# Residual and branch sum of a streaming-encoder layer: vector adds against accumulating DMAs

## The chip, the cores and the metric

The kernel runs on one core of one Trainium2 chip. A core has a matrix engine (TensorE, in the profile PE, with PEld for its weight loads), a vector engine (VectorE, DVE), a scalar engine (ScalarE, ACT), GpSimd (POOL), and SyncE (SP), which here only issues DMAs. They run side by side, each through its own queue in order, and wait for each other on semaphores. Matmul results land in PSUM, everything else lives in SBUF (128 partitions), inputs and outputs in HBM. The metric is the device time of one execution in microseconds.

## The reference

One layer of a hybrid encoder over 1024 prompt frames and 32 sample frames, 1056 tokens of 1024 features, all in float32:

```python
h = rmsnorm(x, g_mix)
q, k, v, cb, cc, cx, ga, gc = split(h @ w_in)
y_attn = attend(q, k, v) @ w_attn_out
y_conv = (cb * causal_conv(cc * cx)) @ w_conv_out
merged = sigmoid(ga) * y_attn + sigmoid(gc) * y_conv     # the sum of the two branches
x = x + merged @ w_o                                     # the residual of the output projection
f = square(relu(rmsnorm(x, g_ffn) @ w_up)) @ w_down
x = x + f
x = x + sigmoid(rmsnorm(x, g_ple) @ w_ple_gate) * (p @ w_ple)
y = rmsnorm(x, g_final)
```

Keys, values and the last convolution rows are outputs as well.

## The kernel before

All activations are held transposed: a row block is 128 features on the partitions by 1056 tokens, and there are KD = 8 such rows of the model width. A float32 matmul is made of three passes: operands are split into a high part (a cast on ScalarE) and a low part (a subtraction on VectorE), and high x high, high x low and low x high are accumulated in PSUM. The tokens are taken in three thirds of 352 columns (`ts`), one PSUM bank each.

Stages in order: input projection, attention, the branch projections, the output projection, the MLP up and down, the gated embedding. The change lies in the branch projections (`branches`, line 1022) and the output projection (`output_projection`, line 1401).

`branches` goes over 14 units, the list SEQ_B: c2, a0, c3, a1, c4, a2, c5, a3, c6, a4, c7, a5, a6, a7, where a is the attention branch, c the convolution branch and the number is the row. (c0 and c1 were done during attention.) A unit loads its weights and its gate two units ahead (`branch_fetch`, SP's queue), splits the weights one unit ahead (`branch_high` on ScalarE, `branch_low` on VectorE), runs three groups of 12 matmuls, one for each third (`branch_group`), and multiplies each group by the gate out of PSUM (`branch_post`, line 939, VectorE). The gates of most rows are scaled and put through a sigmoid a unit ahead (`branch_scale`, on GpSimd for c and on VectorE for a; `branch_sigmoid`, ScalarE). The third group of a unit is multiplied during the next unit.

When both branches of a row n are there, that is in the unit after a_n, the row is merged: `merge_add` adds the attention tile into `mg[n]`, `merge_high` casts the sum into `mh[n]`, `merge_low` makes `ml[n]`. The last row is merged in thirds, the first two of them in the last unit. The output projection then reads `mh` and `ml` of all eight rows.

`output_projection` goes over the 8 output rows, with three groups of 24 matmuls each (`wo_group`, lines 1379 to 1381); for row 0 the contributions of input rows 0 to 6 come first, those of row 7 at the end. `wo_fetch(n)` (SP's queue) loads the weights and the residual rows of x two rows ahead, `wo_post` adds the residual to each group out of PSUM, and `wo_after` stores the finished row (SP), makes the operands of the MLP (`operands`: two scalings on ScalarE, two subtractions on VectorE), squares the row (ScalarE) and adds the square to a running sum (GpSimd). `wo_sums` builds sums of two rows for the MLP's Strassen-like products and stores them (SP).

The order of instructions on TensorE, ScalarE, VectorE and GpSimd is the order of the calls inside a hand-ordered block; `branches` and `output_projection` stand in one such block. The order of SP's queue, and how neighbouring blocks meet, is left to a scheduler when the program is built. Tiles of a row come from a common pool of 34 buffers (`blk`), which are reused when their last reader is done.

Of the kernel before, what the change touches and what calls it, by code (L numbers as in the profile page):

```python
# [17 lines left out]
KD = D // P  # L18
# [4 lines left out]
NTT = 3  # L23
# [25 lines left out]
def tile_step(  # L49
# [8 lines left out]
    nc = tc.nc  # L58
# [7 lines left out]
    def blk(name, dt=F32, shape=None):  # L66
        return bpool.tile(shape or [P, T], dt, tag="B", name=name)

    ts = [slice(t * TT, (t + 1) * TT) for t in range(NTT)]
# [26 lines left out]
    def raw_w(w, n, kb, name):  # L96
        raw = wraw.tile([P, kb, P], F32, tag="raw", name=f"raw_{name}")
        nc.sync.dma_start(raw, w[n])
        return raw
# [36 lines left out]
    add, sub = ALU.add, ALU.subtract  # L136
    dve, pool = nc.vector.tensor_tensor, nc.gpsimd.tensor_tensor
# [5 lines left out]
    def group(name, n=TT):  # L143
        if spare_ps:
            return spare_ps.pop(0)[:, :n]
        p_ = pools[turn[0] % len(pools)]
        turn[0] += 1
        return p_.tile([P, 384], F32, tag="g", name=name)[:, :n]
# [26 lines left out]
    def prepare_plain(s_, i):  # L175
        w = load_w(None, 0, KD, f"{s_}_{i}", raw=raws[s_][i])
        ws.setdefault(s_, {}).update(zip(("A21", "A22") if i else ("A11", "A12"), even_odd(w)))
# [714 lines left out]
    full = [slice(0, T)]  # L892
    oh, ol, mg, mh, ml = [], [], [], [], []

    fetched, made = {}, {}

    def branch_fetch(b):
        nm, n = b
        w = raw_w(w_conv_out if nm == "c" else w_attn_out, n, 4, f"o{nm}{n}")
        sg = blk(f"s{nm}{n}")  # L900
        nc.sync.dma_start(sg, gd[n + (8 if nm == "c" else 0)])
        fetched[b] = w, sg

    def branch_high(b):
        nm, n = b
        hi = wsp.tile([P, 4, P], F32R, tag="whi", name=f"whi_o{nm}{n}")
        nc.scalar.copy(hi, fetched[b][0])
        made[b] = hi

    def branch_low(b):  # L910
        nm, n = b
        lo = wsp.tile([P, 4, P], F32R, tag="wlo", name=f"wlo_o{nm}{n}")
        dve(lo, fetched[b][0], made[b].bitcast(F32), op=sub)
        made[b] = made[b], lo
# [4 lines left out]
    def branch_scale(b):  # L919
        if gate_ready(b):  # L920
            return
        sg = fetched[b][1]
        (pool if b[0] == "c" else dve)(sg, sg, rs, op=ALU.mult)

    def branch_sigmoid(b):
        if gate_ready(b):
            return
        nc.scalar.activation(fetched[b][1], fetched[b][1], AF.Sigmoid)

    def branch_group(b, t):  # L930
        nm, n = b
        if t == 0 and nm == "c":
            mg.append(blk(f"mg{n}"))
        made[b, t] = ps = group(f"ps_o{nm}{n}_{t}")
        gemm(ps, made[b], 0, *((ch, cl) if nm == "c" else (oh, ol)), ts[t])

    def branch_post(b, t):
        sg = fetched[b][1][:, ts[t]]
        dve(mg[b[1]][:, ts[t]] if b[0] == "c" else sg, made.pop((b, t)), sg, op=ALU.mult)

    def merge_add(n, c):
        dve(mg[n][:, c], mg[n][:, c], fetched["a", n][1][:, c], op=add)

    def merge_high(n, c):
        if len(mh) == n:
            mh.append(blk(f"mh{n}", F32R))
            ml.append(blk(f"ml{n}", F32R))
        nc.scalar.copy(mh[n][:, c], mg[n][:, c])

    def merge_low(n, c):  # L950
        dve(ml[n][:, c], mg[n][:, c], mh[n][:, c].bitcast(F32), op=sub)
# [70 lines left out]
    def branches():  # L1022

        seq = SEQ_B
        for i, b in enumerate(seq):
            prev, nxt = seq[i - 1] if i else None, seq[i + 1] if i + 1 < len(seq) else None
            if i + 2 < len(seq):
                branch_fetch(seq[i + 2])
            else:
                wo_fetch(i + 2 - len(seq))  # L1030
            done = prev and prev[0] == "a"
            if nxt:
                branch_high(nxt)
            else:
                wo_high(0)
            branch_group(b, 0)
            if prev:
                branch_post(prev, 2)
            if done:
                merge_add(prev[1], full[0])  # L1040
                merge_high(prev[1], full[0])
            if nxt:
                branch_scale(nxt)
                branch_low(nxt)
                branch_sigmoid(nxt)
            else:
                wo_low(0)
            if done:
                merge_low(prev[1], full[0])
            branch_group(b, 1)  # L1050
            branch_post(b, 0)
            if nxt is None:
                merge_add(b[1], ts[0])
                merge_high(b[1], ts[0])
                merge_low(b[1], ts[0])
            branch_group(b, 2)
            branch_post(b, 1)
            if nxt is None:
                merge_add(b[1], ts[1])
                merge_high(b[1], ts[1])  # L1060
                merge_low(b[1], ts[1])
# [19 lines left out]
    place, done = min(hooks), 0.0  # L1081
# [27 lines left out]
    with tc.manual_schedule(engines=MM):  # L1109
        nc.scalar.preload_act_table_set("sqrt_and_others")  # L1110
        run(first_gates())
        for s_ in range(2, len(SETS)):
            nm, n = SETS[s_]
# [239 lines left out]
    def fetch_up(s_):  # L1353
        fetch_pair(f"u{s_}", w_up, 2 * s_)

    wo, xs = {}, {}

    def wo_fetch(n):
        xs[n] = blk(f"xr{n}")
        wo[n] = raw_w(w_o, n, KD, f"wo{n}")  # L1360
        nc.sync.dma_start(xs[n], xf[n])

    def wo_high(n):
        hi = wsp.tile([P, KD, P], F32R, tag="whi", name=f"whi_wo{n}")
        nc.scalar.copy(hi, wo[n])
        wo[n] = wo[n], hi

    def wo_low(n):
        raw, hi = wo[n]
        lo = wsp.tile([P, KD, P], F32R, tag="wlo", name=f"wlo_wo{n}")  # L1370
        dve(lo, raw, hi.bitcast(F32), op=sub)
        wo[n] = hi, lo

    def wo_group(n, t, ks, ps=None):
        if ps is None:
            ps = wo[n, t] = group(f"ps_wo{n}_{t}")
        (hi, lo), c = wo[n], ts[t]
        for k in ks:
            nc.tensor.matmul(ps, hi[:, k, :], mh[k][:, c], start=k == 0, stop=False, skip_group_check=True)
            nc.tensor.matmul(ps, hi[:, k, :], ml[k][:, c], start=False, stop=False, skip_group_check=True)  # L1380
            nc.tensor.matmul(ps, lo[:, k, :], mh[k][:, c], start=False, stop=k == KD - 1, skip_group_check=True)

    def wo_post(n, t):
        dve(xs[n][:, ts[t]], wo.pop((n, t)), xs[n][:, ts[t]], op=add)

    def wo_after(n):

        x1.append(xs[n])
        nc.sync.dma_start(xd[n], xs[n])
        operands(n)  # L1390
        q = ssq1 if n == 0 else blk(f"sq{n}")
        nc.scalar.square(q, xs[n])
        if n:
            (dve if n == KD - 1 else pool)(ssq1, ssq1, q, op=add)

    def wo_sums(n):
        if n % 2 and n < KD - 1:
            for k, src in sums(n // 2, x1[n - 1], x1[n]).items():
                nc.sync.dma_start(td["T1 T2 T3 T4".split().index(k)][n // 2], src)

    def output_projection():

        for n in range(KD):
            if n + 2 < KD:
                wo_fetch(n + 2)
            else:
                fetch_up(n + 2 - KD)
            if n + 1 < KD:
                wo_high(n + 1)
            else:  # L1410
                prepare_plain("u0", 0)
            if n == 0:
                branch_post(("a", KD - 1), 2)
                for t in range(NTT):
                    wo_group(0, t, range(KD - 1))
                merge_add(KD - 1, ts[2])
                merge_high(KD - 1, ts[2])
                merge_low(KD - 1, ts[2])
                wo_low(1)
                for t in range(NTT):  # L1420
                    wo_group(0, t, [KD - 1], wo[0, t])
                    wo_post(0, t)
                continue
            wo_group(n, 0, range(KD))
            if n > 1:
                wo_post(n - 1, 2)
            if n + 1 < KD:
                wo_low(n + 1)
            wo_after(n - 1)
            wo_group(n, 1, range(KD))  # L1430
            wo_post(n, 0)
            wo_sums(n - 1)
            wo_group(n, 2, range(KD))
            wo_post(n, 1)
        wo_post(KD - 1, 2)
        wo_after(KD - 1)
# [469 lines left out]
    with tc.manual_schedule(engines=MM):  # L1906
        branches()
        output_projection()

    with tc.manual_schedule(engines=MM):  # L1910
# [99 lines left out]
        for u in range(8, 24):  # L2010
# [8 lines left out]
            t = u // 8 - 1  # L2019
# [75 lines left out]
```

## Time and profile before

| | |
|---|---|
| median of 3 runs | 1542.54 us (1541.74 to 1542.68) |
| profiled execution, whole time | 1542.94 us |
| its span | 1541.1 us |
| TensorE busy | 1522.7 us (99%) |
| VectorE, ScalarE, GpSimd busy | 1056.5 (69%), 747.3 (48%), 335.1 us (22%) |
| HBM read, written | 186.31 MB, 80.72 MB |
| mean granted TensorE clock | 0.997 |

The span is the time from the first to the last instruction that the profiler records; the whole time lies 1.84 us above it. In a row of the timeline the first number is the start in us, the second the busy time, then engine, line, operation, tiles written and read with their shapes, and in brackets the idle time before it and what ended that. Of a tile or line, a row gives count and shortest, median and longest duration in ns. A window row gives its ends and length, then busy time and instruction count of PE, PEld, DVE, ACT and POOL, the granted clock, the share of the DMA engines and GB/s. A DMA row gives count, size and the median us from issue to landing.

### The profile page before, as it was taken

To read this page: it belongs to the slowest core of one execution; us is meant where nothing else is said; L and a number is where in the kernel's file an instruction comes from. 1 tells how busy PE (TensorE), PEld (TensorE's weight loads), DVE (VectorE), ACT (ScalarE), POOL (GpSimd) and SP (SyncE) were. 2 spreads that over 40 slices of the span, in tenths; PEclk is the share of its full clock that TensorE was granted. 3 is DMA by queue.
4 is the path that set the end of the run, shared out by engine and by line. 5 is a ranking of instruction groups with operands and counts; after the bars stand their busy time and mean duration, and the time that the engine had idled before them with its cause. 6 is when DMAs were issued, how large, how long until landed. Compare 5 with 4: busy or idle time off the path is not lost. (4 is left out here: it accounts for less than half of the span.)

```text
span 1541.1 us, 29464 instructions
## 1 busy us (share of the span) xinstructions
PE 1522.7 (99%) x11840; PEld 1511.4 (98%) x11840; DVE 1056.5 (69%) x1425; ACT 747.3 (48%) x1367; POOL 335.1 (22%) x342
## 2 busy tenths in 40 slices
PE   8999999999999999999999999999999999999997
PEld 8999999999999999999999999999999999999997
DVE  7568656656777887665577555445577986789756
ACT  6544444434555664322365555555643334434654
POOL 2123322230222232101312222222020220000253
PEclk9999999999999999999999999999999999999999
DMA  6513545415644843354354343444886897683443
GB/s 221 202 53 111 192 153 193 166 45 182 197 117 151 281 141 133 133 180 176 121 188 152 140 154 137 142 148 154 290 289 199 286 326 237 210 273 122 138 129 117
DMA packets 110569, 268.96 MB, mean 175 GB/s; under 512 B 12992, under 2 KB 30144, under 8 KB 110432
## 3 DMA queue, kind: packets, MB, share of 16 engines
q1 hardware_dynamic: 110144, 266.75, 51.2%
q8 instruction: 93, 1.52, 0.4%
q14 instruction: 44, 0.36, 0.1%
q10 hardware_dynamic: 288, 0.32, 0.1%
HBM read 186.31 MB, written 80.72 MB: 173 GB/s over the span
## 5 line engine op out<-in xcount | busy, mean ns | idle before, releaser
L1690 PE MATMUL ps_dn<-fh,whi_dn 128*128 128x264 f32 x896 | 254.7, 284 | 0.0
L1691 PE MATMUL ps_dn<-fl,whi_dn 128*128 128x264 f32 x896 | 254.5, 284 | 0.0
L1692 PE MATMUL ps_dn<-fh,wlo_dn 128*128 128x264 f32 x896 | 254.5, 284 | 0.0
L1692 PEld LDWEIGHTS ps_dn<-fh,wlo_dn 128*128 128x128 f32 x896 | 168.7, 188 | 0.0
L1691 PEld LDWEIGHTS ps_dn<-fl,whi_dn 128*128 128x128 f32 x896 | 168.5, 188 | 0.0
L1690 PEld LDWEIGHTS ps_dn<-fh,whi_dn 128*128 128x128 f32 x896 | 168.5, 188 | 0.0
L809 DVE TENSOR_TENSOR_SCAN r<-r 128x128 f32<-128x128 f32 (+3 forms) x64 | 86.6, 1353 | 5.6 <-POOL r L802 5.6
L203 POOL TENSOR_TENSOR s_i<-raw_i,raw_i 128x512 f32<-128x512 f32 x30 | 41.2, 1372 | 223.7 <-DVE slS_i L166 194.0
L203 POOL TENSOR_TENSOR s_u<-raw_u,raw_u 128x512 f32<-128x512 f32 x30 | 44.1, 1471 | 184.6 <-DVE slS_u L166 184.4
L1577 ACT CAST whi_dn<-raw_dn 128x1024 fp32r<-128x1024 f32 x40 | 42.1, 1051 | 84.7 <-PE ps_dn L1691 84.7
L802 POOL TENSOR_SCALAR_AFFINE_SELECT r<-r 128x128 f32<-128x128 f32 x64 | 40.1, 627 | 192.1 <-ACT r L795 192.1
L1583 DVE TENSOR_TENSOR wlo_dn<-raw_dn,whi_dn 128x1024 fp32r<-128x1024 f32 x40 | 61.3, 1531 | 28.5 <-ACT whi_dn L1577 28.5
L1774 POOL TENSOR_TENSOR xx<-xx,pgs 128x384 f32<-128x384 f32 (+1 forms) x23 | 24.3, 1058 | 216.4 <-DVE pgs L1773 209.8
L1603 DVE TENSOR_TENSOR fl<-mr,fh 128x1056 fp32r<-128x1056 f32 x56 | 70.0, 1249 | 0.3 <-ACT q L1643 0.3
L849 DVE TENSOR_TENSOR at<-pa,at 128x512 fp32r<-128x512 f32 (+2 forms) x96 | 51.9, 550 | 24.7 <-ACT at L848 24.2
L216 PE MATMUL ps_A11u<-T,shS_u 128*128 128x264 f32 x240 | 68.4, 285 | 0.0
L218 PE MATMUL ps_A11i<-T,slS_i 128*128 128x264 f32 x240 | 68.4, 285 | 0.0
L217 PE MATMUL ps_A11u<-T,shS_u 128*128 128x264 f32 x240 | 68.3, 285 | 0.0
L216 PE MATMUL ps_A11i<-T,shS_i 128*128 128x264 f32 x240 | 68.3, 285 | 0.0
L217 PE MATMUL ps_A11i<-T,shS_i 128*128 128x264 f32 x240 | 68.2, 284 | 0.0
L218 PE MATMUL ps_A11u<-T,slS_u 128*128 128x264 f32 x240 | 68.0, 283 | 0.0
L166 DVE TENSOR_TENSOR slS_i<-s_i,shS_i 128x512 fp32r<-128x512 f32 x45 | 36.1, 806 | 45.4 <-ACT shS_i L164 45.1
(451 smaller groups left out, 5607.8 us busy)
## 6 DMA issues: line engine op xcount, KB each, us to landing
raw_dn<-in_w_down_dram SPq DMA_DIRECT2D x56, 512.0 KB, 4.6
raw_i<-in_w_in_dram SPq DMA_DIRECT2D x34, 512.0 KB, 4.5
mr<-mdT SPq DMA_DIRECT2D x32, 528.0 KB, 5.7
raw_u<-in_w_up_dram SPq DMA_DIRECT2D x32, 512.0 KB, 3.6
mdB<-m SPq DMA_DIRECT2D x48, 264.0 KB, 2.4
mr<-mdB SPq DMA_DIRECT2D x24, 528.0 KB, 6.4
raw_pg<-in_w_ple_gate_dram SPq DMA_DIRECT2D x17, 512.0 KB, 3.6
mdT<-ta SPq DMA_DIRECT2D x32, 264.0 KB, 2.1
```

Source lines behind the costliest of these rows:

```text
L203: f()
L216: nc.tensor.matmul(p_, wh[:, k, :], o[:, 0, c], start=new and n == 0, stop=False, **on)
L217: nc.tensor.matmul(p_, wh[:, k, :], o[:, 1, c], start=False, stop=False, **on)
L218: nc.tensor.matmul(p_, wl[:, k, :], o[:, 0, c], start=False, stop=z, **on)
L809: nc.vector.tensor_tensor_scan(rev, rev, rev, 1.0, ALU.mult, ALU.bypass)
L849: nc.vector.tensor_tensor(al, pt[:, :nb, :], ah.bitcast(F32), op=ALU.subtract)
L1577: nc.scalar.copy(hi, dws[u])
L1583: dve(lo, raw, hi.bitcast(F32), op=sub)
L1603: dve(l, mraw.pop(v), opd[v].bitcast(F32), op=sub)
L1690: nc.tensor.matmul(ps, hi[:, j, :], oh, start=j == 0, stop=False)
L1691: nc.tensor.matmul(ps, hi[:, j, :], ol, start=False, stop=False)
L1692: nc.tensor.matmul(ps, lo[:, j, :], oh, start=False, stop=j == NP_ - 1)
```

## The change

Four edits. `merge_add` of rows 0 to 6 becomes a DMA from SBUF to SBUF, issued by GpSimd, that adds the attention tile into `mg[n]`; row 7 keeps the vector add. In `branches`, `merge_high` moves from before the second group to after the first multiplication, and `merge_low` from before the second group to after the second multiplication. The residual of the output rows 0 to 6 is no longer loaded ahead: `wo_post` copies the group out of PSUM on ScalarE, and after the third copy a DMA issued by GpSimd adds the row of x from HBM into the tile; row 7 keeps the load and the vector add. In `output_projection`, `wo_after` moves behind the second group and its post, and `wo_sums` behind the third group.

```diff
     def merge_add(n, c):
-        dve(mg[n][:, c], mg[n][:, c], fetched["a", n][1][:, c], op=add)
+        if n < KD - 1:
+            nc.gpsimd.dma_start(mg[n][:, c], fetched["a", n][1][:, c], accum_op=add)
+        else:
+            dve(mg[n][:, c], mg[n][:, c], fetched["a", n][1][:, c], op=add)
...
             if done:
                 merge_add(prev[1], full[0])
-                merge_high(prev[1], full[0])
             if nxt:
                 branch_scale(nxt)
                 branch_low(nxt)
                 branch_sigmoid(nxt)
             else:
                 wo_low(0)
-            if done:
-                merge_low(prev[1], full[0])
             branch_group(b, 1)
             branch_post(b, 0)
+            if done:
+                merge_high(prev[1], full[0])
             if nxt is None:
                 merge_add(b[1], ts[0])
                 merge_high(b[1], ts[0])
                 merge_low(b[1], ts[0])
             branch_group(b, 2)
             branch_post(b, 1)
+            if done:
+                merge_low(prev[1], full[0])
...
         wo[n] = raw_w(w_o, n, KD, f"wo{n}")
-        nc.sync.dma_start(xs[n], xf[n])
+        if n == KD - 1:
+            nc.sync.dma_start(xs[n], xf[n])
...
     def wo_post(n, t):
-        dve(xs[n][:, ts[t]], wo.pop((n, t)), xs[n][:, ts[t]], op=add)
+        if n == KD - 1:
+            dve(xs[n][:, ts[t]], wo.pop((n, t)), xs[n][:, ts[t]], op=add)
+            return
+        nc.scalar.copy(xs[n][:, ts[t]], wo.pop((n, t)))
+        if t == NTT - 1:
+            nc.gpsimd.dma_start(xs[n], xf[n], accum_op=add)
...
                 wo_low(n + 1)
-            wo_after(n - 1)
             wo_group(n, 1, range(KD))
             wo_post(n, 0)
+            wo_after(n - 1)
+            wo_group(n, 2, range(KD))
             wo_sums(n - 1)
-            wo_group(n, 2, range(KD))
             wo_post(n, 1)
```

## The prediction

> **What bounds the kernel now.** I read the page first, then busy time by windows, then TensorE's waits, then the timelines of TensorE, VectorE and ScalarE around the places the change touches. The page gives the frame:
>
> ```profile
> span 1541.1 us, 29464 instructions
> ...
> PE 1522.7 (99%) x11840; PEld 1511.4 (98%) x11840; DVE 1056.5 (69%) x1425; ACT 747.3 (48%) x1367; POOL 335.1 (22%) x342
> ```
>
> TensorE is busy for 1522.7 of 1541.1 us; 18.4 us of idle time is all there is to win. A window over the end of the branch projections and the start of the output projection, and the longest wait of TensorE in the whole run:
>
> ```profile
> 660.00:680.00 20.00, 20.00 (x126) 20.00 (x125) 13.96 (x21) 6.25 (x8) 0.00 (x0) 1.00 0.50 170
> ```
>
> ```profile
> PE ps_g L216 <- ACT B L342: 6.1, 1, 6.1
> ```
>
> In this window TensorE (first number after the length) has no gap: 20.00 of 20.00. The longest wait is the one before its first matmul, and no wait stands at a changed line. So VectorE time saved here buys nothing, and the change can show only where a later result makes TensorE wait. The question is how late the accumulated rows come.
>
> **The merge: what is removed and added.** Seven merge adds leave VectorE (lines 941-942), seven accumulating DMAs go to GpSimd's queue. The tightest place is the last two, rows 5 and 6, just before the output projection reads row 6. TensorE, VectorE and ScalarE there, before:
>
> ```profile
> 669.43 0.32 PE L118 MATMUL ps_oa<-o3h,wlo_oa 128*128 128x352 f32 x1
> ...
> 675.42 0.32 PE L1379 MATMUL ps_wo<-mh,whi_wo 128*128 128x352 f32 x1
> ...
> 678.51 0.32 PE L1380 MATMUL ps_wo<-ml,whi_wo 128*128 128x352 f32 x1
> ```
>
> ```profile
> 664.01 0.53 DVE L939 TENSOR_TENSOR sa<-ps_oa,sa 128x352 f32<-128x352 f32 x1 [1.43 <-PE ps_oa L118]
> ...
> 669.80 0.53 DVE L939 TENSOR_TENSOR sa<-ps_oa,sa 128x352 f32<-128x352 f32 x1 [0.66 <-PE ps_oa L118]
> 670.36 1.26 DVE L942 TENSOR_TENSOR mg<-mg,sa 128x1056 f32<-128x1056 f32 x1
> 671.53 1.22 DVE L1371 TENSOR_TENSOR wlo_wo<-raw_wo,whi_wo 128x1024 fp32r<-128x1024 f32 x1
> 672.77 1.26 DVE L951 TENSOR_TENSOR ml<-mg,mh 128x1056 fp32r<-128x1056 f32 x1
> ```
>
> ```profile
> 669.68 1.06 ACT L1365 CAST whi_wo<-raw_wo 128x1024 fp32r<-128x1024 f32 x1 [2.70 <-PE ps_oa L117]
> 671.65 1.09 ACT L948 CAST mh<-mg 128x1056 fp32r<-128x1056 f32 x1 [0.91 <-DVE mg L942]
> 675.05 0.49 ACT L948 CAST mh<-mg 128x352 fp32r<-128x352 f32 x1 [2.32 <-DVE mg L942]
> ```
>
> The output projection starts at 675.42; of the seventh of its eight input rows (row 6) the low part is first read at 678.51, the high part one matmul earlier. Before, the low part of row 6 was written by 672.77 + 1.26 = 674.03: 4.5 us of slack. I call L the time from the end of the last multiplication (line 939), which releases the DMA, to the start of the cast (merge_high) that waits for it. Engine orders are written out by hand inside this block, so I walk them:
>
> Row 5: released at 664.01 + 0.53 = 664.54. Its cast starts at 664.54 + L and takes 1.08. VectorE's merge_low of row 5 now stands after two of the next row's multiplications, but ahead of the third: it ends at 664.54 + L + 1.08 + 0.03 + 1.26 = 666.9 + L. The third multiplication (0.53), which releases row 6, ends at 667.45 + L; that is later than the 670.33 of before (669.80 + 0.53) once L is over 2.9.
>
> Row 6: its cast runs from 667.45 + 2L to 668.53 + 2L. Queued behind it on ScalarE is the first third of row 7's cast, 0.49 (its add on VectorE, a third of 1.26, is ready earlier, after the 1.22 of the weight's low part and 0.53 of a multiplication). It ends at 669.02 + 2L. VectorE then waits in the first third of row 7's merge_low, put at the 0.53 of another third-width operation, to 669.6 + 2L; multiplies, to 670.1 + 2L; and only then makes the low part of row 6, to 671.4 + 2L. TensorE needs it at 678.5. The stall is **2L - 7.1**, nothing below L = 3.55, and 2 us for each us of L, since the wait is taken twice in one chain.
>
> **What L is.** No row shows a DMA of GpSimd's queue or an accumulating one. The nearest rows, from issue to landing:
>
> ```profile
> mdT<-ta SPq DMA_DIRECT2D x32, 264.0 KB, 2.1
> ...
> xr<-in_xf_dram SPq DMA_DIRECT2D x8, 528.0 KB, 4.6
> xd<-xr SPq DMA_DIRECT2D x8, 528.0 KB, 2.9
> ...
> x<-in_xf_dram SPq DMA_DIRECT2D x4, 528.0 KB, 8.2
> ```
>
> Lower end: a plain transfer of this size out of SBUF, 2.9, if reading the destination is free. Upper end: a load of this size in the crowded first stage, 8.2. In between, 264 KB more cost 2.9 - 2.1 = 0.8, so reading the 528 KB destination as well costs about 1.6 more: 4.5 on top of the store, 6.2 on top of the load. Source and destination are both on the core and the DMA engines are half free (0.50 in the window above), which is nearer to the store. I take L = 5.0 as an estimate: stall 2 x 5.0 - 7.1 = 2.9 us. Ends: nothing at 2.9, 9.3 us at 8.2.
>
> The Trainium skill, page "DMA: Bandwidth & Descriptors", section "Anatomy of one DMA — SWDGE (gpsimd) path", gives for a GpSimd DMA about 2.0 us plus bytes over 436 GB/s, for 540,672 bytes an estimate of 3.24 us. By it the stall would be nothing; the page says nothing there of an accumulate, and no run here yet shows which holds.
>
> **What a stall brings with it.** The same trace has one place where TensorE's clock falls inside the kernel, right after two short waits at line 791. TensorE's waits between 376 and 392, and windows of 1 us (the clock stands after the POOL column):
>
> ```profile
> PE z L791 <- ACT r L795: 0.9, 1, 0.9
> PE z L791 <- issue: 0.5, 1, 0.5
> ```
>
> ```profile
> 385.00:386.00 1.00, 1.00 (x8) 1.00 (x7) 0.42 (x1) 0.38 (x1) 0.35 (x2) 0.68 0.81 330
> 386.00:387.00 1.00, 1.00 (x6) 0.90 (x5) 0.69 (x1) 0.02 (x1) 0.00 (x0) 0.50 1.08 397
> 387.00:388.00 1.00, 1.00 (x6) 1.00 (x6) 0.34 (x2) 1.00 (x6) 0.47 (x3) 0.50 0.89 260
> 388.00:389.00 1.00, 1.00 (x6) 0.81 (x5) 0.82 (x1) 0.09 (x1) 0.11 (x1) 0.61 0.82 204
> ```
>
> Lost work: 0.32 + 0.50 + 0.50 + 0.39 = 1.7 us, after 1.4 us of waiting. A stall of 2.9 us should bring the same: I add 1.7. Ends: 0, and 1.7 once.
>
> The Trainium skill, page "TensorE: Matmul & The Clock Gate", section "Part 1: The HAM clock gate", has the clock halved only after an idle window of about 3.4 us. By that, 2.9 us would keep the full clock and the sum would be 2.9 alone; the trace disagrees, with two waits of 0.5 and 0.9 us.
>
> **The rest of the edit, costed at nothing, with its cover.** Rows 0 to 4 merge every second unit (a unit is one 128-row branch projection, 675.42 - 669.6 = 5.8 us). The rows that follow carry these and the output projection's part:
>
> ```profile
> 629.11 0.52 DVE L939 TENSOR_TENSOR sa<-ps_oa,sa 128x352 f32<-128x352 f32 x1 [1.43 <-PE ps_oa L118]
> ```
>
> ```profile
> 639.66 2.48 POOL L923 TENSOR_TENSOR sc<-sc,rs 128x1056 f32<-128x1056 f32 x1 [9.83 <-DMA sc<-gd]
> ```
>
> ```profile
> 646.96 1.08 ACT L928 ACTIVATE sc<-sc 128x1056 f32<-128x1056 f32 x1
> ```
>
> ```profile
> L1384 DVE TENSOR_TENSOR xr<-ps_wo,xr x24: 511/524/527, 686.3 to 768.9; 128x352 f32<-128x352 f32 x24
> L1323 ACT ACTIVATE B<-xr,vecT x16: 721/730/740, 688.1 to 770.3; 128x528 fp32r<-128x528 f32 x16
> L1324 DVE SCALAR_TENSOR_TENSOR B<-xr,vecT,B x16: 753/762/771, 689.4 to 771.6; 128x528 fp32r<-128x528 f32 x16
> ```
>
> ```profile
> 757.05 1.05 ACT L107 CAST whi_u<-raw_u 128x1024 fp32r<-128x1024 f32 x1 [7.75 <-PE ps_wo L1380]
> ```
>
> ```profile
> 768.67 0.28 PE L216 MATMUL ps_up<-B,whi_u 128*128 128x264 f32 x1
> 768.79 0.29 PE L217 MATMUL ps_up<-B,whi_u 128*128 128x264 f32 x1
> ```
>
> Row 2: released at 629.63, merge_low ends at 632.0 + L, the blocked multiplication takes 0.53, the next weight's low part about 0.7 (half of the 1.22 for 1024 columns, and a little): ready at 633.2 + L. TensorE reads it two units on, about 628.9 + 11.7 + 0.3 = 640.9. Cover up to L = 7.7; beyond that each of the five rows pays the excess. On GpSimd the gate scaling of 639.66 now queues behind a DMA that is released only two units after row 2's, at 629.63 + 11.7 = 641.3; even with 1 us for the issue it ends by 644.8, and its reader on ScalarE (sigmoid) ran at 646.96.
>
> Output projection: 21 residual adds of 0.524 (11.0 us) leave VectorE, 21 copies of about 0.5 (the 0.49 of a cast of 352 columns) join ScalarE, which is busy for 6.25 of 20 us: covered. Seven loads leave SP's queue and come back as accumulates, each released when the row's last copy is done. Worst is row 6: weight cast at 757.05, 1.05 long, copy 0.5, so the DMA starts at 758.6. With 4.6 + 1.6 = 6.2 it lands at 764.8, two scalings of 0.73 and a square follow to about 767.3. The projection up starts at 768.67, one matmul each 0.12, and reads rows 6 and 7 only after 36 matmuls, at 773.0: cover for 12 us of landing; row 7's own operands, whose last part starts at 771.6, keep their place if row 6 lands within 8.5. SP's stores of each finished row (line 1389) wait about 6 us longer, and the weight loads queued behind them are fetched two rows, 23 us, ahead. The sums of moved line 1432 come about 8 us later, still before the loads that read them back after row 7. If all this cover were gone, each us late would cost one.
>
> **Sum.** Stall 2.9 + slow clock 1.7 + nothing else = 4.6. Against the profiled execution, 1541.1 span and 1542.94 in all: 1545.7 and 1547.5. The median shown is 0.4 below that execution, so 1542.5 + 4.6 = **1547.1**.
>
> **Rivals.** (1) The transfer is quick, L at or under 3.9: for it, the 2.9 of the store; against it, a second read and a new queue. Stall at most 0.7 us and no clock loss: 1542.5 to 1543.2, not slower. The border to slower lies near L = 4.3, where the stall is 1.5 and with the slow clock 3.2. (2) The accumulate is slow, L over 7.7: for it, the 8.2 row; against it, that row lies in a stage with all DMA engines busy. At 8.2: 9.3 + 1.7 at the end, 5 x 0.5 in the rows before: 1556. (3) Faster: scheduling of SP's queue and of the borders between hand-ordered blocks, which is not written out by hand, closes one of the gaps in the 18.4 us; a gap of 1.4 us with its clock loss of 1.7 is 3.1: 1539.4. Nothing in the changed lines feeds it. (4) Stall without clock loss: 1545.4.
>
> **Chances.** Forecast with (4), L between 3.9 and 7.7: 0.58 (its own range, L from 4.5 to 6.2: 1544.4 to 1549.5); (1) 0.25; (2) 0.13; (3) 0.04. Changes within 0.2%, 3.1 us, cannot be told from none: (1), and 0.10 of the forecast's share (L near 4) count there. So faster 0.04, same 0.35, slower 0.61. Range 1542.0 to 1553.0: it leaves out (3) and most of (2).
>
> **What would show it.** In the changed trace, 14 transfers of 528 KB issued from GpSimd, whose time from issue to landing gives L. TensorE should wait at line 1380 for `ml` of row 6, about 3 us, with the clock at 0.50 for some 3.4 us after it, and wait at no other changed line. VectorE should sit idle ahead of the row-5 merge_low and then ahead of row 7's first one, each time for ScalarE's cast, which waits for a DMA. Wrong: no wait at line 1380; a wait at line 118 in a unit before it (L over 7.7); a wait at lines 216 to 218 after the output projection (the residual lands too late).

## The result and the profile after the change

| | before | after |
|---|---|---|
| median of the runs | 1542.57 us | 1558.62 us (1557.43 to 1560.36) |
| ratio, 95% interval | | 1.0105 (1.0093 to 1.0117) |
| span of the profiled execution | 1541.1 us | 1556.0 us |

The kernel became 1.05% slower. The page of the changed kernel:

```profile
span 1556.0 us, 29479 instructions
...
PE 1528.8 (98%) x11840; PEld 1515.4 (97%) x11840; DVE 1044.9 (67%) x1397; ACT 755.5 (49%) x1388; POOL 345.9 (22%) x356
```

VectorE does 11.6 us less work (1056.5 before) and TensorE stands still longer: 27.2 us of the span instead of 18.4; its busy time grew too, by 6.1 us, though it runs the same 11,840 matmuls. TensorE's largest waits (line, what it waited for, total, times, longest) of the changed kernel that the kernel before has not:

```profile
PE ps_wo L1384 <- ACT mh L951: 3.3, 1, 3.3
PE ps_up L217 <- DVE B L1328: 2.4, 1, 2.4
PE ps_wo L1385 <- DVE ml L954: 1.9, 1, 1.9
...
PE ps_wo L1386 <- DVE wlo_wo L1376: 0.5, 1, 0.5
```

The matmuls stand in the same order in both traces, so each can be set against its twin. How much later it starts after the change:

```
place in the kernel                              start before   later by
last branch unit                                 668.2 us       -0.1 us
output projection, just past its row 6           680.6           8.3
output projection, half way                      743.8           8.0
projection up, just past its first reads         775.5          12.2
last projection                                  1492.4         14.8
last matmul                                                     14.9
```

There are two steps, of 8.3 and 4.2 us, and a slow slope of 2.7 us over the MLP, whose code is the same in both. Ahead of the change the differences cancel: the changed kernel is 1.1 us late by 384 us, and gains 1.5 us where the kernel before has its clock dip and the changed one has none.

**The first step** is the place that the prediction walked through. VectorE, ScalarE and GpSimd of the changed kernel there:

```profile
663.74 1.38 DVE L939 TENSOR_TENSOR sa<-ps_oa,sa 128x352 f32<-128x352 f32 x3
...
673.35 1.26 DVE L954 TENSOR_TENSOR ml<-mg,mh 128x1056 fp32r<-128x1056 f32 x1 [5.08 <-ACT mh L951]
674.52 0.52 DVE L939 TENSOR_TENSOR sa<-ps_oa,sa 128x352 f32<-128x352 f32 x1
...
683.58 1.25 DVE L954 TENSOR_TENSOR ml<-mg,mh 128x1056 fp32r<-128x1056 f32 x1
```

```profile
672.24 1.08 ACT L951 CAST mh<-mg 128x1056 fp32r<-128x1056 f32 x1 [8.01 <-DMA mg<-sa]
...
681.21 1.46 ACT L951 CAST mh<-mg 128x1056 fp32r<-128x1056 f32 x2 [6.94 <-DMA mg<-sa]
```

```profile
665.42 0.86 POOL L943 DMA_DIRECT2D mg<-sa  x1 [11.00 <-DVE sa L939]
675.34 0.86 POOL L943 DMA_DIRECT2D mg<-sa  x1 [9.06 <-DVE sa L939]
```

Row 5 is released at 663.74 + 1.38 = 665.12 and cast at 672.24: L = 7.12. VectorE stands 5.08 us in front of its low part, and the multiplication behind it, which releases row 6, ends at 675.04 instead of 670.33. Row 6 is cast at 681.21: L = 6.17. Its low part ends at 683.58 + 1.25 = 684.83; TensorE wanted it at 678.5, so it is 6.3 us late. The three waits make 5.7 us. After them the clock is halved (windows with busy time and count of each engine, clock, DMA share):

```profile
680.00:684.00 4.00, 0.66 (x1) 0.29 (x1) 1.30 (x3) 1.46 (x2) 0.00 (x0) 0.78 0.35 127
684.00:686.00 2.00, 1.12 (x4) 1.12 (x5) 1.45 (x3) 0.70 (x2) 0.00 (x0) 0.50 0.00 0
686.00:688.00 2.00, 2.00 (x9) 2.00 (x8) 1.42 (x4) 1.21 (x2) 0.00 (x0) 0.50 0.01 4
688.00:690.00 2.00, 2.00 (x11) 2.00 (x11) 1.54 (x2) 0.00 (x0) 0.00 (x0) 0.73 0.00 0
...
785.00:787.00 2.00, 2.00 (x11) 2.00 (x10) 1.96 (x3) 1.46 (x4) 0.00 (x0) 0.50 0.89 318
787.00:789.00 2.00, 2.00 (x15) 2.00 (x14) 1.97 (x4) 0.99 (x2) 0.00 (x0) 0.73 0.92 365
```

TensorE's busy time in the first four windows at the clock it had (the one matmul of the first at half) lost 0.33 + 0.56 + 1.00 + 0.54 = 2.4 us. Waits and clock make 8.1 of the 8.3.

**The second step** lies where the projection up first reads rows 6 and 7. GpSimd, ScalarE and then VectorE of the changed kernel:

```profile
761.96 1.53 POOL L203 TENSOR_TENSOR s_u<-raw_u,raw_u 128x512 f32<-128x512 f32 x1 [5.98 <-DMA raw_u<-in_w_up_dram]
...
766.66 1.30 POOL L203 TENSOR_TENSOR s_u<-s_u,raw_u 128x512 f32<-128x512 f32 x1
767.91 2.47 POOL L1404 TENSOR_TENSOR ssq<-ssq,sq 128x1056 f32<-128x1056 f32 x1
770.32 0.86 POOL L1394 DMA_DIRECT2D xr<-in_xf_dram  x1
780.04 2.44 POOL L1404 TENSOR_TENSOR ssq<-ssq,sq 128x1056 f32<-128x1056 f32 x1 [8.86 <-ACT sq L1402]
```

```profile
765.94 0.45 ACT L1392 COPY xr<-ps_wo 128x352 f32<-128x352 f32 x1
776.20 0.74 ACT L1327 ACTIVATE B<-xr,vecT 128x528 fp32r<-128x528 f32 x1 [9.81 <-DMA xr<-in_xf_dram]
...
782.51 0.73 ACT L1327 ACTIVATE B<-xr,vecT 128x528 fp32r<-128x528 f32 x1 [1.05 <-POOL ssq L1404]
```

```profile
773.39 1.22 DVE L108 TENSOR_TENSOR wlo_u<-raw_u,whi_u 128x1024 fp32r<-128x1024 f32 x1
...
780.85 2.71 DVE L108 TENSOR_TENSOR wlo_u<-raw_u,whi_u 128x1024 fp32r<-128x1024 f32 x1 [0.90 <-ACT whi_u L107]
783.49 1.44 DVE L1328 SCALAR_TENSOR_TENSOR B<-xr,vecT,B 128x528 fp32r<-128x528 f32 x2
```

The third copy of row 6 ends at 765.94 + 0.45 = 766.39, and from then on the residual's DMA could go. But GpSimd issues it only at 770.32: it runs its instructions in order, and in front of the DMA stand four sums over the weight of the projection up (line 203, which began late because they waited for the weight's own load) and the sum of squares of the row before (line 1404). (In the kernel before, the sum of squares of row 5 stood ahead of these four sums, from 748.76 us, and they began at 751.43.) ScalarE waits to 776.20, and the weight's cast and row 7's operands come behind. There the low part of the weight takes 2.71 us on VectorE instead of 1.22, while GpSimd adds the square of row 6 (780.04 to 782.48), and row 7's first operand, which TensorE waits for, stands behind it. At 1.22 us that operand would have been there at about 780.85 + 1.22 + 0.77 = 782.8 instead of 784.3, so by this estimate 1.4 of TensorE's 2.4 us at line 217 are that. The last two windows above lose 1.00 + 0.54 us to the clock.

### The profile page after: what moved, and what is told of

The parts are those of the page before. It is cut to its first block, busy times and chain, and to the rows that moved or that the text cites. A ratio compares the mean times of both kernels' runs of the same rounds, so it can differ in the third digit from the quotient of the medians.

```text
span 1556.0 us, 29479 instructions
## 1 busy us (share of the span) xinstructions
PE 1528.8 (98%) x11840; PEld 1515.4 (97%) x11840; DVE 1044.9 (67%) x1397; ACT 755.5 (49%) x1388; POOL 345.9 (22%) x356
```

## The experiments

Each was compared with the kernel before on the same chip. "Junction" is the first step above. All diffs are against the kernel before unless another is named.

**The two halves of the change, and its moves without its DMAs.** The first kernel has only the sum of the branches by DMA, with the moves that belong to it:

```diff
 def merge_add(n, c):
+    if n < KD - 1:
+        nc.gpsimd.dma_start(mg[n][:, c], fetched["a", n][1][:, c], accum_op=add)
+    else:
...
-                merge_high(prev[1], full[0])
...
-            if done:
-                merge_low(prev[1], full[0])
             branch_group(b, 1)
             branch_post(b, 0)
+            if done:
+                merge_high(prev[1], full[0])
...
             branch_group(b, 2)
             branch_post(b, 1)
+            if done:
+                merge_low(prev[1], full[0])
```

> The branch sum by accumulating DMAs and the moved merge_high and merge_low, the residual as before. Theory: TensorE waits once, at the first read of row 6 in the output projection, because two DMA landings stand in one chain; matmul by matmul the changed kernel lost 8.3 us there (wait 6.4, slow clock 1.9), so about 1551, and no wait at lines 216 to 218 when the MLP starts. Rival (the two edits are only slow together, through GpSimd's queue or the DMA engines): within 3 us of before.

The second has only the residual by DMA:

```diff
-        nc.sync.dma_start(xs[n], xf[n])
+        if n == KD - 1:
+            nc.sync.dma_start(xs[n], xf[n])
...
+        nc.scalar.copy(xs[n][:, ts[t]], wo.pop((n, t)))
+        if t == NTT - 1:
+            nc.gpsimd.dma_start(xs[n], xf[n], accum_op=add)
...
-            wo_after(n - 1)
             wo_group(n, 1, range(KD))
             wo_post(n, 0)
-            wo_sums(n - 1)
+            wo_after(n - 1)
             wo_group(n, 2, range(KD))
+            wo_sums(n - 1)
```

> The residual by accumulating DMAs with wo_after and wo_sums moved, the branch sum as before. Theory: the row-6 DMA is issued late on GpSimd, behind the MLP's weight sums and a square sum, and the MLP waits for operands: the 4.4 us that the changed kernel lost there, so about 1547. Rival (that loss follows from the stall of the branch sum, which shifts the loads): under 1 us, 1542.5 to 1543.5. The slow drift of 2.5 us through the MLP that the changed kernel showed: if it comes from the residual DMAs it stays here, if it is the run, it goes.

The third keeps both additions on VectorE and the residual loaded ahead, and makes only the moves, those of `merge_high` and `merge_low` in the first diff and those of `wo_after` and `wo_sums` in the second.

> All moved calls, but the adds on VectorE and the residual loaded ahead, as before the change: no DMA from GpSimd. Theory (the DMAs' latency makes the loss, the moves alone have slack): 1542 to 1544. Rival (the later casts and sums cost by themselves): above 1545.

| kernel | median, us | kernel before, us | ratio, 95% interval |
|---|---|---|---|
| sum of the branches only | 1554.44 | 1542.11 | 1.0079 (1.0062 to 1.0095) |
| residual only | 1547.21 | 1542.11 | 1.0037 (1.0024 to 1.0050) |
| moves only | 1543.45 | 1542.11 | 1.0009 (1.0000 to 1.0019) |

The two halves make 1.16% against 1.05% together, within the intervals, and the moves as such have no new wait but one of 0.3 us in the MLP. With the sum of the branches only, TensorE waits at the junction and no more at the projection up:

```profile
PE ps_wo L1383 <- ACT mh L951: 3.5, 1, 3.5
PE ps_wo L1384 <- DVE ml L954: 2.1, 1, 2.1
PE ps_wo L1385 <- DVE wlo_wo L1375: 1.0, 1, 1.0
```

Its 1554.44 us are 3 more than the 1551 expected: L was longer here, 7.71 and 6.43 us on rows 5 and 6, the junction cost 9.8 us instead of 8.3, and the slope over the MLP is there too.

With the residual only, the one new wait is at the projection up, 2.4 us, and the clock stays full. GpSimd of that kernel; the third copy of row 6 ended at 758.48:

```profile
758.66 1.28 POOL L203 TENSOR_TENSOR s_u<-s_u,raw_u 128x512 f32<-128x512 f32 x1
759.90 2.46 POOL L1400 TENSOR_TENSOR ssq<-ssq,sq 128x1056 f32<-128x1056 f32 x1
762.30 0.87 POOL L1390 DMA_DIRECT2D xr<-in_xf_dram  x1
```

So the DMA stands 3.8 us in GpSimd's queue here too, where nothing had been delayed before.

**Breaking the chain at the junction.** If two landings in one chain are the cause, it is enough that VectorE doesn't stand in front of row 5's low part before it releases row 6. The edit also puts row 6's low part ahead of row 7's first third. Against the kernel with the sum of the branches only; the transfers stay:

```diff
             if done:
                 merge_add(prev[1], full[0])
+            if nxt is None:
+                merge_low(5, full[0])
...
+            if nxt is None:
+                merge_low(6, full[0])
             if nxt is None:
                 merge_add(b[1], ts[0])
...
-            if done:
+            if done and prev[1] < 5:
                 merge_low(prev[1], full[0])
```

> As merge_only, but VectorE's merge_low of row 5 stands after the multiplication that releases row 6, and merge_low of row 6 ahead of row 7's first merge: the same DMAs, the two landings no longer in one chain. Theory: row 6 is released at about 670.3 instead of 675.0, its low part is ready near 679.3 against the 678.5 where it is read: a stall of about 1 us, 1543 to 1545. Rival (the loss comes from the DMA traffic or GpSimd, not from the order on VectorE): as merge_only, about 1551.

Measured: 1544.88 us, 1.0018 (1.0009 to 1.0028) instead of 1.0079. VectorE of this kernel:

```profile
669.30 0.52 DVE L939 TENSOR_TENSOR sa<-ps_oa,sa 128x352 f32<-128x352 f32 x1 [1.43 <-PE ps_oa L118]
673.57 1.26 DVE L954 TENSOR_TENSOR ml<-mg,mh 128x1056 fp32r<-128x1056 f32 x1 [3.74 <-ACT mh L951]
...
677.19 1.26 DVE L954 TENSOR_TENSOR ml<-mg,mh 128x1056 fp32r<-128x1056 f32 x1 [0.79 <-ACT mh L951]
```

Row 6 is released at 669.82, 6.4 us sooner than with the sum of the branches only (676.25); its landing runs beside row 5's wait, and its low part ends at 678.45 (677.19 + 1.26). L of the two rows is no shorter (7.73 and 6.26 us). At the junction TensorE waits only for a weight's low part, 0.6 us, and the clock stays full. The transfer's length alone costs little; its place in the chain costs most of the first step.

**What the transfer's time consists of.** Two kernels replace the accumulating DMA by a plain copy of the attention tile, so the sum of the two branches is left out for rows 0 to 6. One issues it from GpSimd, against the kernel with the sum of the branches only, the other from SyncE:

```diff
-            nc.gpsimd.dma_start(mg[n][:, c], fetched["a", n][1][:, c], accum_op=add)
+            nc.gpsimd.dma_start(mg[n][:, c], fetched["a", n][1][:, c])
...
+            nc.sync.dma_start(mg[n][:, c], fetched["a", n][1][:, c])
```

> As merge_only, but the seven DMAs from GpSimd copy the attention tile over the row instead of adding it: the sum of the two branches is left out for rows 0 to 6. In merge_only rows 0 and 1, beside which no other transfer ran, took 1.5 us from issue to first packet and 2.8 to 2.9 us from the first packet to the last end. Theory (an accumulate reads its destination as well and so moves twice the bytes): the packets take about half, 1.4 to 1.6 us, each packet clearly under the 340 ns of the accumulate. Rival (the time lies in GpSimd's queue): 1.5 and 2.8 as before.

> The same copies without the add, issued by SyncE instead of GpSimd. What GpSimd's queue itself costs is the difference to the copies issued by GpSimd in the time from issue to first packet: theory, 0.3 to 0.8 us less than 1.5; rival, no difference (the start belongs to the transfer).

Measured: 1546.0 and 1542.83 us, one run each, against 1542.8. Issues of the change, then of the copy by GpSimd, then by SyncE (count, size, median us from issue to landing; "sc" is the tile of rows 0 and 1):

```profile
mg<-sa POOLq DMA_DIRECT2D x5, 528.0 KB, 6.8
...
sc<-sa POOLq DMA_DIRECT2D x2, 528.0 KB, 4.7
```

```profile
mg<-sa POOLq DMA_DIRECT2D x5, 528.0 KB, 4.0
sc<-sa POOLq DMA_DIRECT2D x2, 528.0 KB, 3.0
```

```profile
mg<-sa SPq DMA_DIRECT2D x5, 528.0 KB, 3.3
sc<-sa SPq DMA_DIRECT2D x2, 528.0 KB, 3.0
```

On rows 0 and 1, where hardly another packet ran beside, the accumulate lands 1.7 us later than the copy from the same queue. The packets say why: one of 4,224 bytes takes 336 to 376 ns in the accumulate and 161 to 176 in the copy, and all of them 2.8 to 2.9 us instead of 1.45 to 1.5. That fits the second read that the prediction priced at 1.6 us. The queue costs less: from the release to the cast a GpSimd copy takes 3.6 us on the quiet rows and a SyncE copy 3.0. The difference isn't where it was expected. From issue to first packet the two take nearly the same, 1.16 to 1.29 and 1.13 to 1.17 us on rows 0 to 2; but GpSimd starts the issue 0.56 to 0.62 us after the release and SyncE 0.02 to 0.03. By the walk of the prediction the GpSimd copy, with L of 4.35 and 4.10 on rows 5 and 6, should stall TensorE by 4.35 + 4.10 - 7.1 = 1.35 us; it waits 0.8 us for that low part. The SyncE copy (3.36 and 4.25, 0.5 by the walk) makes no new wait; the walk is some 0.45 us too long, as is worked out below. With seven adds less on VectorE this one run is still not faster than the kernel before: nothing was to be won there.

**Other traffic beside the transfer.** Rows 3 to 6 landed later than rows 0 to 2. To see whether other transfers do that, the kernel with the sum of the branches only got extra stores of the attention tile, into memory that nobody reads, beside rows 0 and 1; first one, then three:

```diff
+    spill = dpool.tile([6, P, T], F32, name="spill")
...
             nc.gpsimd.dma_start(mg[n][:, c], fetched["a", n][1][:, c], accum_op=add)
+            if n < 2:
+                for i in range(3):
+                    nc.sync.dma_start(spill[3 * n + i], fetched["a", n][1])
```

> As merge_only, and for rows 0 and 1 SyncE also stores the attention tile (528 KB) to a scratch row in HBM that nobody reads, released by the same multiplication as the accumulate. In merge_only nothing ran beside these two: 2.8 and 2.9 us from the first packet to the last, 5.3 us from the release to the cast; rows 3 to 5 had 0.5 to 0.9 MB of other traffic beside them and took 4.7 to 4.9, and 7.3 to 7.8 to the cast. Theory (the traffic that falls beside them makes the difference): rows 0 and 1 now take 4.2 to 5 us and 6.5 to 7.5 to the cast. Rival (the later rows are slow for another reason): 2.8 and 5.3 as before. The time, about 1554, is not what is asked.

> As extra_store, with three stores of 528 KB instead of one beside each accumulate of rows 0 and 1. The one store landed 2.7 us after its issue, before the accumulate's packets began, and told nothing. Three keep the DMA engines busy for about 4 us, into the accumulate. Theory (traffic beside it makes an accumulate late): its packets take 4 us or more instead of 2.8, and the cast starts 6.3 or more after the release. Rival: 2.8 and 5.3.

The single store told nothing: SyncE issued it sooner, it had landed in 2.7 us, about when the accumulate's packets began, and L was 5.47 and 5.68 (1553.39 us, one run). Three did it. Issues and TensorE's waits of that kernel (1560.02 us, one run):

```profile
sc<-sa POOLq DMA_DIRECT2D x2, 528.0 KB, 8.5
```

```profile
PE ps_oc L118 <- DVE wlo_oc L913: 2.6, 4, 1.2
```

With 0.71 and 0.76 MB of other packets running beside it, row 0's L went from 5.27 to 8.92 us and row 1's from 5.29 to 9.33; the first packet came 3.0 to 3.2 us after the issue (1.5 to 1.6 in the change) and the packets took 5.0 and 5.3 us. In the change itself rows 0 to 2 had 0 to 0.02 MB beside them and L of 5.28 to 5.41; rows 3 to 5 had 0.52 to 0.72 MB, packets that took 4.3 to 4.5 us and L of 7.12 to 7.50; row 6 had 0.23 MB and 6.17. The packets of rows 3 to 5 were no longer for it, 336 ns in the median: other packets stood between them. This run also shows the cover of the earlier rows used up: L is 1.2 and 1.6 us over the 7.7 of the prediction, and TensorE now waits 3.5 us in the branch units (2.6 at the line shown), 1.0 us where row 0's excess arrives and 1.9 where row 1's does. No other kernel of the study waits more than 0.2 us there.

**The residual: GpSimd's queue or its sums.** With the residual only, the square sums of rows 5 and 6 go to VectorE; the weight sums stay:

```diff
-            (dve if n == KD - 1 else pool)(ssq1, ssq1, q, op=add)
+            (dve if n >= 5 else pool)(ssq1, ssq1, q, op=add)
```

> As resid_only, but the square sums of rows 5 and 6 are added on VectorE instead of GpSimd, so that nothing but the weight sums of the MLP stands before the DMA of row 6 on GpSimd. In resid_only that DMA was free to start at 758.5 and issued at 762.3, and TensorE waited 2.4 us at line 217. Theory (the queue on GpSimd delays row 6): issue near 760, the wait falls under 0.5 us, 1542.5 to 1544.5. Rival (the wait is the landing time itself, or the moved calls): the 2.4 us stay, about 1547.

Measured: 1544.92 us, 1.0014 (1.0005 to 1.0023) instead of 1.0037; TensorE's wait at line 217 fell from 2.4 to 0.7 us. GpSimd of this kernel:

```profile
758.06 2.18 POOL L203 TENSOR_TENSOR s_u<-s_u,raw_u 128x512 f32<-128x512 f32 x1
760.18 0.88 POOL L1390 DMA_DIRECT2D xr<-in_xf_dram  x1
```

The time and the 0.7 us lie a little above what was expected. The DMA goes 2.1 us sooner, right behind the last weight sum. But the edit takes away more: VectorE's wait of 6.3 us for GpSimd's sum of row 5, and GpSimd's sum of row 6, beside which the weight's low part took 2.71 us (1.21 here). The run doesn't part these. It shows that GpSimd's sums make the loss; what the DMA's place behind them costs alone isn't shown.

**Does the freed VectorE bring anything?** In the change, the DMAs of the last rows are taken back: sums of rows 0 to 4 and residuals of rows 0 to 5 stay DMAs.

```diff
     def merge_add(n, c):
-        if n < KD - 1:
+        if n < 5:
...
         wo[n] = raw_w(w_o, n, KD, f"wo{n}")
-        if n == KD - 1:
+        if n >= KD - 2:
...
     def wo_post(n, t):
-        if n == KD - 1:
+        if n >= KD - 2:
```

> The whole change with its last rows taken out: the branch sum by DMA for rows 0 to 4, the residual by DMA for rows 0 to 5, VectorE for the others. Theory (only the rows whose result is read at once make TensorE wait; VectorE's saved time is worth nothing): no wait at a changed line, within 0.2% of before, 1541 to 1545. Rival (DMAs from GpSimd slow the rest): above 1546. If the saved vector time is worth something after all: under 1539.

Measured: 1546.55 us, 1.0024 (1.0015 to 1.0034). That is over the 1545 of the theory and on the side of the rival. No wait is left at the junction, but 1.8 us are lost at the projection up (lines 216 and 217 wait 0.6 us each), and 2.1 us are the slope over the MLP. Row 6 has no DMA here, and is late all the same. GpSimd and VectorE of this kernel:

```profile
761.10 2.48 POOL L1404 TENSOR_TENSOR ssq<-ssq,sq 128x1056 f32<-128x1056 f32 x1
```

```profile
763.61 0.77 DVE L155 SCALAR_TENSOR_TENSOR w<-xr,vecT 128x528 f32<-128x528 f32 x1 [6.36 <-POOL ssq L1404]
...
771.44 2.73 DVE L108 TENSOR_TENSOR wlo_u<-raw_u,whi_u 128x1024 fp32r<-128x1024 f32 x1
```

The sum of squares of row 5 still stands behind the four weight sums on GpSimd. VectorE waits 6.36 us for it, and the adds of row 6 come behind, from 766.58 instead of 758.36 before. So at the second place it is GpSimd's order that costs, with or without a DMA of row 6. The additions of eleven rows off VectorE bring nothing.

**Both repairs in the whole change.** All fourteen DMAs, the reordered low parts, and the square sums on VectorE:

```diff
+            if nxt is None:
+                merge_low(5, full[0])
...
+            if nxt is None:
+                merge_low(6, full[0])
...
-            if done:
+            if done and prev[1] < 5:
                 merge_low(prev[1], full[0])
...
-            (dve if n == KD - 1 else pool)(ssq1, ssq1, q, op=add)
+            (dve if n >= 5 else pool)(ssq1, ssq1, q, op=add)
```

> The whole change, all fourteen DMAs, with both repairs of order: VectorE's merge_low of rows 5 and 6 placed as in late_low, the square sums of rows 5 and 6 on VectorE as in resid_sq. Theory (the loss is two places where something else queues in front of a late DMA): the sum of the two repaired halves, 0.18% and 0.14% over before, so 1545 to 1548. Rival (the two halves together lose more than apart, through the DMA engines): above 1550. Faster than before, below 1540, by no theory.

Measured: 1545.94 us, 1.0023 (1.0014 to 1.0033). Two edits that leave every transfer in place take back 0.82 of the 1.05%. No version was faster than the kernel before.

**The kernel before once more**, unchanged, to see how far two profiles of one program differ in clock and in the slope:

> The kernel before, unchanged, profiled once more on this chip. The changed kernels run behind the first profile of before by 1 to 2.5 us that grow evenly over the MLP stages, where nothing is changed. Theory (executions and chips differ in that): this profile too grows apart from the first by 0.5 us or more over the MLP. Rival (the change slows later matmuls): under 0.2 us. Second, whether the half clock after the two waits in attention (0.9 and 0.5 us) shows up again in the same code.

Its span is 1540.7 us. The clock dip at 385 us on which the prediction built its second term isn't there, though line 791 waits the same 0.9 and 0.5 us (the same windows as in the prediction):

```profile
385.00:386.00 1.00, 1.00 (x10) 0.96 (x8) 0.51 (x2) 0.38 (x1) 0.29 (x1) 1.00 1.07 427
386.00:387.00 1.00, 1.00 (x10) 0.95 (x9) 0.70 (x3) 0.91 (x6) 0.35 (x2) 1.00 1.01 300
```

Of the fourteen profiles here, five have that dip and nine don't, all with these two waits. The slope isn't there either. From 830 to 1400 us, over most of the MLP, none of the 4,686 steps from one matmul to the next differs by more than 0.001 us between the two profiles of the kernel before; two short delays, at 1416.6 and 1422.6, then make 0.3 us, which lies between the 0.5 and the 0.2 of the two theories but is no even growth. With the moves only, 1,728 of the same steps differ by more than 0.003 us. So the even growth isn't scatter between executions, as far as two can show; it goes with the changed programs.

## Why the prediction was right in its direction and too small

It said 4.6 us and a median of 1547.1; the profile grew by 14.9 and the median by 16.05, past the end of its range. Two of its steps failed: L, taken as 5.0 us, was 7.12 and 6.17, and the residual, put at nothing, cost 4.2 us.

**TensorE is the bound and nothing is to be won.** Right. The kernels that freed VectorE with few or no new waits of TensorE (the last rows taken back, copies by SyncE) gained nothing.

**The chain 2L - 7.1.** The mechanism is right, and the run that broke the chain shows it. The term that was mis-sized is L: 5.0 was taken, 7.12 and 6.17 measured. With these the walk gives 7.12 + 6.17 - 7.1 = 6.2, and the low part came 6.3 us late. That match hides two small errors: row 4's landing had already put off row 5's release by 0.6 us (665.12 for 664.54), a third link that the walk left out, and the walk put 0.45 us too much on the way from a cast to the next release and low part. The sign named was a wait for the low part; 3.3 us of the wait came one matmul earlier, for the high part, and 0.5 us at a weight's low part delayed on VectorE. For a quiet row the estimate was good (5.0 for 5.28 to 5.41). What failed is the reading "the DMA engines are half free": 0.50 was a mean over 20 us. Windows of 2 us inside that stretch, of the kernel before (the DMA share is the last number but one):

```profile
664.00:666.00 2.00, 2.00 (x14) 2.00 (x14) 1.96 (x3) 0.56 (x2) 0.00 (x0) 1.00 0.00 0
...
676.00:678.00 2.00, 2.00 (x14) 2.00 (x13) 1.41 (x4) 0.87 (x2) 0.00 (x0) 1.00 1.01 395
```

The engines were free or taken, by turns. The transfers of rows 3 to 5 met a weight load or a gate tile each time. By the Trainium skill, page "DMA: Bandwidth & Descriptors", section "Anatomy of one DMA — SWDGE (gpsimd) path", the estimate for one such DMA was 3.24 us; the quiet copy from GpSimd, 3.0, comes near it, and the quiet accumulate, 4.7, doesn't.

**The slow clock.** Its place is right, its size isn't: 2.4 us for 1.7. A second dip, of 1.5 us at the projection up, wasn't forecast. And the premise that a dip follows a wait is too simple: the dip at 385 us is missing in the second profile of the same program and in the changed kernel; a 2.4 us wait at line 217 was followed by one in the change and by none with the residual only. The Trainium skill, page "TensorE: Matmul & The Clock Gate", section "Part 1: The HAM clock gate", calls the window free-running and 3,413 ns long. The clock records of the changed trace agree in the length, with half-clock stretches of 6,827 ns at the junction and 3,413 ns at the projection up; that a whole idle window must come first, they don't bear out: the wait ahead of the second was 2.4 us. Which waits bring a dip stays open.

**Rows 0 to 4 at no cost.** Right: L up to 7.50 and no wait, and a wait once it was pushed to 9. The gate scaling on GpSimd ended in time too. What the walk missed cost nothing there: shifted behind the DMA, the scaling of rows 0 to 2 runs beside a weight's low part on VectorE, which takes 3.40 to 3.62 us instead of 0.68.

**The residual at no cost.** This is the step that failed outright. The landing was priced well (6.2 assumed, 5.9 from issue to cast), but its start, "the DMA starts at 758.6", followed ScalarE's copy alone. With the residual only, the copy ended at 758.48 and the DMA was issued at 762.30. Row 6 then arrived 9.7 us after its copy, beyond the 8.5 that keep row 7's operands in place. The prediction checked GpSimd's queue for what the DMAs delay, not for what delays the DMAs, nor for what GpSimd's later sums run beside. It cost 4.2 us at this place, clock included; the sign it had named for it, a wait at lines 216 to 218, is what came.

**The rivals.** The slow accumulate gave 1556, near the time that came, but not for its reason: its condition, L over 7.7 and waits in the branch units, wasn't met. Stall without clock loss didn't come in the change; the residual alone shows one, at the other place.

**What is left.** 2.7 us of the 14.9 are the slope over the MLP, which the prediction didn't have. From 830 to 1400 us of the kernel before, TensorE fell behind the first profile by 0.0 us (the kernel before again), 1.0 (moves only, and copies by SyncE), 1.1 to 2.0 (the eight other kernels with accumulates), 1.9 (copies by GpSimd) and 2.1 (the change). It comes evenly, at full recorded clock, and also where GpSimd issues no DMA. It goes with the program, but what in it makes it wasn't found; it may account for a part of the 0.14 to 0.24% that the repaired kernels still lose.

## What to carry to other kernels

Before an addition goes to a DMA, count how often its latency stands in one chain: an engine that waits for one landing ahead of the instruction that releases the next pays each twice, and moving that one instruction took back most of the loss here. Ask of a DMA not only what it delays but what stands in front of it in its issuer's queue, and what else in that queue comes later with it. Price its landing from windows as short as the transfer, at the very time at which it will run; a mean share of the DMA engines over a stage hides the transfer that will run beside it.

## What the hardware showed beyond that

An accumulating packet of 4,224 bytes took 336 to 376 ns beside no other traffic, a copying one 161 to 176, though both ends are on the core. Issuing one 528 KB DMA kept GpSimd itself busy for 0.85 to 1.02 us, and the first packet came 1.45 to 1.6 us after a quiet issue, 1.9 to 2.3 us on rows 3 to 5, which had traffic beside them. VectorE's low parts of the weights (subtractions with both inputs in SBUF) all but stood still while GpSimd ran a sum or a scaling. From 600 to 800 us the changed kernel has 22 of them. The fifteen with none beside them took 0.68 to 0.69 us (512 columns) or 1.22 to 1.23 (1024). The seven others ran beside one for 0.55 to 2.78 us and took 0.41 to 2.94 us longer, each by 0.7 to 1.1 of the time that they ran beside it. No run tested this by itself, but no low part is an exception.
